# Linear attention: one PSUM tile of four banks for the scores of four heads, and one masked copy of 512 columns

## The chip, the cores and the metric

The kernel runs on one core of a Trainium2 chip. The metric is the device time of one execution in microseconds. Five engines work side by side, each through its own instruction queue in order: PE (TensorE, matrix products, with its weight loads shown apart as PEld), DVE (VectorE), ACT (ScalarE), POOL (GpSimd) and SP (SyncE, which issues most transfers). An engine waits for another by asking for a value of that engine's counter; whatever stands behind the waiting instruction in its queue waits too.

## The reference

One step of a two-layer backbone. Each layer normalises its input, multiplies it by one input projection, and feeds three groups of heads (a state-space group with a convolution, "SSD"; a gated linear attention, "GLA"; a windowed attention), whose outputs pass one output projection. 17 tiles of 128 tokens go through it: 16 of latent tokens and one of context tokens ("CT"). The change sits in the linear attention, where within a chunk of 64 tokens

```python
tri = jnp.tril(jnp.ones((GLA_CHUNK, GLA_CHUNK), dtype=bool))[None, None, None]
att = jnp.where(tri, jnp.einsum('bcqhd,bcshd->bchqs', q_in, k_in), 0.0)
o_intra = jnp.einsum('bchqs,bcshv->bcqhv', att, v)
```

for 4 heads, in two directions.

## The kernel before

Per layer there are four stages. **GLA** (`gla_group`, line 513) takes groups of two tiles: projections into the PSUM pool "d", then gates, cumulative sums and exponentials on DVE and ACT, then for each tile the scores of four heads (L589, 16 small matmuls), their masked copy to SBUF (L590), the sum of the two directions (L591) and the product with the values (L596). **Attention** (`att_weights`, L842) computes per tile four heads of scores (L854, L856), each followed by a maximum on DVE (L857); after the four, exponentials on ACT (L872). **SSD** interleaves by hand the steps of `ssd_scan` for a tile (decays L1104, masked copy L1105, exponential L1107; states L1123 with their reads L1126 and L1133; outputs L1144 and L1151 with their reads L1152 and, after an addition on POOL at L1153, L1154) with the blocks of `ssd_conv` for the next group: 24 matmuls of the helper `prod` (L281), a first tap on ACT (L1057) and four taps on DVE (L1059). Two convolution blocks in four go into the pool "d", two into the pool "s". **Output** (`out_tile`, L1181) forms a gate product in pool "s", which ACT (L1192) and DVE (L1193) read, and the output products in pool "d".

PSUM has eight banks: pools "d" and "m" with two tiles each and "s" with four. `psum(shape, "s")` serves all four stages: every call makes a new tile in one of the four buffers. Waits are not written in the program. The layer that builds it records which instruction touches which tile, derives the waits, and sets the order on every engine from them by a plan of its own; so a change of what depends on what moves instructions everywhere.

Of the kernel before, what the change touches and what calls it, by code (L numbers as in the profile page):

```python
# [10 lines left out]
F32 = mybir.dt.float32  # L11
# [9 lines left out]
P = 128  # L21
# [57 lines left out]
def hybrid_kernel(ctx, tc, a, o):  # L79
    nc = tc.nc  # L80
    V, S, G, T, D = nc.vector, nc.scalar, nc.gpsimd, nc.tensor, nc.sync
# [9 lines left out]
    psp = ctx.enter_context(tc.tile_pool(name="ps", bufs=1, space=PSUM))  # L91
    drp = ctx.enter_context(tc.tile_pool(name="dr", bufs=1, space=DRAM))

    def view(x, shape, dt=F32):

        n = math.prod(shape[1:])
        if dt in (BF16, F16):
            x = x[0:shape[0], 0:(n + 1) // 2].bitcast(dt)[:, 0:n]
        else:
            x = x[0:shape[0], 0:n]  # L100
        if len(shape) == 3:
            x = x.rearrange("p (a b) -> p a b", a=shape[1])
        elif len(shape) == 4:
            x = x.rearrange("p (a b c) -> p a b c", a=shape[1], b=shape[2])
        elif len(shape) == 5:
            x = x.rearrange("p (a b c d) -> p a b c d", a=shape[1], b=shape[2], c=shape[3])
        return x
# [14 lines left out]
    def rot(xs, key):  # L122
        turn[key] = turn.get(key, -1) + 1
        return xs[turn[key] % len(xs)]

    def sb(tag, shape, dt=F32):
        if tag not in where:
            return small.tile(shape, dt, tag=tag, name=tag, bufs=1 if tag in ONCE else 2)
        ph, off, words, n = where[tag]
        off += words * rot(range(n), tag)  # L130
        return view(home.get(ph, work)[:, off:off + words], shape, dt)

    def arena(x):
# [9 lines left out]

        return take

    def psum(shape=None, tag="m"):
        return psp.tile(shape or [P, 512], F32, tag=tag, name="p" + tag, bufs={"d": 2, "m": 2, "s": 4}[tag])


    K = arena(big.tile([P, C_END + 3348 + 12 + 52 * NTT + 162 * L], F32, name="K"))  # L150
# [6 lines left out]
    gmask = cb[:, C_GM:C_GM + 128].bitcast(I32)  # L157
# [61 lines left out]
    def all_sum(src):  # L219

        pr = psum()
        T.matmul(pr[:, 0:1], lhsT=ones, rhs=src, start=True, stop=True)
        return pr[:, 0:1]
# [67 lines left out]
    def hcol(t):  # L291
        return HC if t == CT else 16 + t * P
# [220 lines left out]
    def gla_group(l, s, g):  # L513
# [6 lines left out]
        h = HT[:, :, :, hcol(tiles[0]):hcol(tiles[0]) + W]  # L520
# [52 lines left out]
        qi = sb("gqi", [P, 2, 256])  # L573
# [3 lines left out]
        ki = sb("gki", [P, 2, 256])  # L577
        V.tensor_tensor(ki[:, :, :W], qk[:, 1:2, :W].to_broadcast([P, 2, W]), e2[:, :, :W], ALU.mult)

        for i, t in enumerate(tiles):  # L580
            ax = rot(s.am, "am")
            tx = rot(s.at, "at")
            for hh in range(4):
                hp = slice(32 * hh, 32 * hh + 32)
                pa = psum([P, 2, 64], "s")
                for d in range(2):
                    for c in range(2):
                        ts = slice(i * P + 64 * c, i * P + 64 * c + 64)
                        T.matmul(pa[64 * c:64 * c + 64, d], lhsT=ki[hp, d, ts], rhs=qi[hp, d, ts], start=True, stop=True)  # L589
                V.copy_predicated(ax[:, hh], gmask.rearrange("p (d s) -> p d s", d=2), pa)  # L590
            V.tensor_tensor(tx, ax[:, :, 0], ax[:, :, 1], ALU.add)  # L591
            po = psum()
            for hh in range(4):
                for c in range(2):
                    cs = slice(64 * c, 64 * c + 64)
                    T.matmul(po[cs, 64 * hh:64 * hh + 64], lhsT=tx[cs, hh], rhs=v[cs, i, 64 * hh:64 * hh + 64], start=True, stop=True)  # L596
            oi = sb("goa", [P, 256])
            S.copy(oi, po[:, 0:256])
            D.dma_start(oacc[t], oi)
            for hh in range(4):  # L600
                D.dma_start(sqin[t][hh // 2, 64 * (hh % 2):64 * (hh % 2) + 64].rearrange("(d k) s -> k d s", d=2), qi[32 * hh:32 * hh + 32, :, i * P:(i + 1) * P])
# [8 lines left out]
        for c in range(2):  # L610
            pst = psum([P, 2, 2, 64])
            cs = slice(64 * c, 64 * c + 64)
            for i in range(n):
                for d in range(2):
                    for hh in range(4):
                        T.matmul(pst[32 * hh:32 * hh + 32, d, i], lhsT=kt[cs, i, d, 32 * hh:32 * hh + 32],
                                 rhs=v[cs, i, 64 * hh:64 * hh + 64], start=True, stop=True)
# [813 lines left out]
def build(shapes, consts):  # L1431
    import concourse.bacc as bacc

    nc = bacc.Bacc("TRN2", target_bir_lowering=False, num_devices=1, dynamic_dma_scratch_size=1024)
    f32 = mybir.dt.from_np(np.dtype("float32"))
    a = {n: nc.dram_tensor(f"in_{n}_dram", s, f32, kind="ExternalInput").ap() for n, s in shapes.items()}
    for n, x in consts.items():
        a[n] = nc.dram_tensor(f"in_{n}_dram", x.shape, f32, kind="ExternalInput").ap()
    depth = shapes["w_in"][0]
    outs = {  # L1440
        "y_prompt": shapes["x_prompt"], "y_sample": shapes["x_sample"],
        "new_cache_k": (1, depth, P, 2, 64), "new_cache_v": (1, depth, P, 2, 64),
        "new_state_ssd": (1, depth, 2, 8, 64, P), "new_state_gla": (1, depth, 2, 4, 32, 64),
    }
    o = {n: nc.dram_tensor(f"out_{i}_dram", outs[n], f32, kind="ExternalOutput").ap() for i, n in enumerate(_OUTS)}
    with tile.TileContext(nc, schedule_with_timeline_sim=True) as tc:
        hybrid_kernel(tc, a, o)
    return nc
# [15 lines left out]
```

## Time and profile before

| | us |
|---|---|
| time, median of 3 runs (lowest, highest) | 2300.2 (2296.73, 2302.02) |
| profiled execution, its time | 2304.28 |
| its span | 2302.5 |
| PE busy | 2080.7 (90%) |
| DVE busy | 1628.4 (71%) |
| ACT busy | 992.4 (43%) |
| POOL busy | 878.6 (38%) |

The stages lie, in the first layer, at about 90 to 335 us (GLA), to 615 (attention), to 930 (SSD) and to 1250 (output); in the second at 1250 to 1435, to 1690, to 2010 and to the end. "PEclk" in the profile is the granted clock of PE, 1.00 for 2.4 GHz and 0.50 for 1.2 GHz.

### The profile page before, as it was taken

What the parts mean: (1) busy time and instruction counts of PE and PEld (TensorE: products, weight loads), DVE (VectorE), ACT (ScalarE), POOL (GpSimd) and SP (SyncE); (2) the same over time, 40 slices, a digit from 0 to 9 for tenths busy, and PEclk for the clock granted to TensorE, in tenths of its full rate; (3) what the DMA queues carried; (4) which work ended last, traced back from release to release, by engine and by line L of the source; (5) the groups of instructions that cost most, each with busy time, mean ns of one, the idle gap of its engine ahead of it and who ended that gap; (6) DMA issues with size and microseconds to landing.
All of it is one profiled execution on the core that took longest, in us unless ns stands there. A gap on an engine that the chain in (4) does not pass through costs nothing. (4 is left out here: it accounts for less than half of the span.)

```text
span 2302.5 us, 53686 instructions
## 1 busy us (share of the span) xinstructions
PE 2080.7 (90%) x21228; PEld 1750.4 (76%) x21245; DVE 1628.4 (71%) x4088; ACT 992.4 (43%) x2185; POOL 878.6 (38%) x918
## 2 busy tenths in 40 slices
PE   2596888999899899998999999899999999989998
PEld 0364767778688788887888887777888778878887
DVE  2465768887599988666665657898779988854442
ACT  2333554665444434433333554666563433422221
POOL 0010015556434354544442003566643344444442
PEclk6797979999899999999999999999999999999999
DMA  8687434576710112676667123556751101265553
GB/s 298 165 263 158 121 103 92 124 154 143 168 58 33 38 38 91 183 199 163 168 160 201 41 69 100 122 125 149 160 139 43 38 33 42 81 182 164 154 146 96
DMA packets 486352, 288.01 MB, mean 125 GB/s; under 512 B 354344, under 2 KB 447924, under 8 KB 483796
## 3 DMA queue, kind: packets, MB, share of 16 engines
q1 hardware_dynamic: 483796, 271.99, 45.4%
q0 software_dynamic: 2304, 12.58, 1.8%
q8 instruction: 167, 2.74, 0.5%
q14 instruction: 85, 0.70, 0.1%
HBM read 141.11 MB, written 64.93 MB: 89 GB/s over the span
## 5 line engine op out<-in xcount | busy, mean ns | idle before, releaser
L281 PEld LDWEIGHTS <-HT 128*128 128x128 f16 x6528 | 583.6, 99 | 128.3 <-issue 50.7
L281 PEld LDWEIGHTS <-slot 128*128 128x128 f16 x4320 | 402.3, 98 | 107.5 <-issue 31.3
L281 PE MATMUL pd<-slot,HT 128*128 128x256 f16 x3456 | 430.8, 279 | 10.3 <-DVE work L728 8.0
L281 PE MATMUL pd<-slot,work 128*128 128x256 f16 x3264 | 366.8, 273 | 8.0 <-DMA work<-work 7.7
L281 PEld LDWEIGHTS <-work 128*128 128x128 f16 x3264 | 319.6, 98 | 50.2 <-DMA work<-work 9.1
L281 PE MATMUL pd<-HT,slot 128*128 128x260 f16 (+3 forms) x2592 | 318.0, 270 | 15.7 <-DMA HT<-work 14.5
L281 PE MATMUL ps<-HT,slot 128*128 128x260 f16 (+1 forms) x1728 | 202.8, 272 | 4.8 <-DVE work L1059 4.8
L281 PE MATMUL ps<-slot,HT 128*128 128x256 f16 x1440 | 169.6, 275 | 17.7 <-ACT work L1192 17.7
L1252 POOL TENSOR_TENSOR work<-work 128x512 f32<-128x512 f32 x68 | 90.1, 1325 | 185.5 <-DVE work L1251 156.2
L875 POOL TENSOR_TENSOR work<-work 128x512 f16<-128x512 f32 (+2 forms) x102 | 123.3, 1211 | 86.0 <-ACT work L874 70.8
L1059 DVE SCALAR_TENSOR_TENSOR work<-ps,work 128x256 f32<-128x256 f32 (+1 forms) x288 | 133.3, 464 | 9.1 <-ACT work L1057 4.6
L793 POOL TENSOR_TENSOR work<-work 128x384 f32<-128x384 f32 x34 | 30.2, 889 | 276.1 <-ACT work L789 174.4
L1059 DVE SCALAR_TENSOR_TENSOR work<-pd,work 128x256 f32<-128x256 f32 (+1 forms) x288 | 132.1, 463 | 3.0 <-ACT work L1057 0.3
L872 ACT ACTIVATE work<-ps,nm,K 128x512 f32<-128x512 f32 (+2 forms) x136 | 100.6, 742 | 54.7 <-DVE nm L864 39.3
L1120 POOL TENSOR_TENSOR work<-work 128x512 f32<-128x512 f32 x68 | 72.3, 1068 | 112.6 <-ACT work L1079 67.6
L1061 ACT ACTIVATE work<-work 128x256 f32<-128x256 f32 (+1 forms) x144 | 58.1, 403 | 123.4 <-DVE work L1059 87.4
L854 PEld LDWEIGHTS <-work 128*128 128x128 f16 x1008 | 71.5, 99 | 41.8 <-issue 34.4
L1218 ACT ACTIVATE work<-work 128x512 bf16<-128x512 f32 x68 | 42.7, 628 | 138.3 <-DMA work<-work 75.5
L1093 POOL TENSOR_TENSOR work<-K,work 128x512 bf16<-128x512 bf16 x68 | 73.5, 1081 | 73.7 <-PE ps L1104 63.8
L874 ACT CAST work<-work 128x512 f16<-128x512 f32 (+2 forms) x136 | 78.0, 586 | 52.3 <-DMA slot<-work 31.4
L281 PE MATMUL pm<-slot,HT 128*128 128x256 f16 x816 | 96.1, 275 | 1.6 <-DVE work L907 1.3
L854 PE MATMUL ps<-work 128*128 128x128 f16 x752 | 76.2, 223 | 21.8 <-DMA work<-work 21.8
(375 smaller groups left out, 4029.2 us busy)
## 6 DMA issues: line engine op xcount, KB each, us to landing
slot<-in_w_in_dram SPq DMA_DIRECT2D x24, 1024.0 KB
ymix<-work SPq DMA_DIRECT2D x68, 128.0 KB
yacc<-work SPq DMA_DIRECT2D x34, 256.0 KB
work<-ymix SPq DMA_DIRECT2D x34, 256.0 KB
work<-yacc SPq DMA_DIRECT2D x34, 256.0 KB
x<-work SPq DMA_DIRECT2D x17, 512.0 KB
work<-x SPq DMA_DIRECT2D x17, 512.0 KB
out_dram<-work SPq DMA_DIRECT2D x17, 512.0 KB
```

The source lines that it names most:

```text
L281: T.matmul(out, lhsT=lhs(i, k), rhs=rhs(j, k), start=(n == 0), stop=(n == 3 * KB - 1))
L793: G.tensor_tensor(sq, x, x, ALU.mult)
L854: T.matmul(ps[:, bs], lhsT=s.qt[t][:, 2 * gg + kv], rhs=kt[:, 2 * kv + j], start=(j == 0), stop=(j == 1 and mk is None))
L872: S.activation(pr, sc[hh][:, :nb * P], AF.Exp, scale=s.isc[:, 0:1], bias=nm[:, hh:hh + 1], accum_out=ls[:, hh:hh + 1])
L874: S.copy(p16[:, 0], pr)
L875: (G if hh else V).tensor_tensor(p16[:, 1], pr, p16[:, 0], ALU.subtract)
L1059: V.scalar_tensor_tensor(acc[:, jj, :W], pp[:, q:q + W], s.cw[j][:, q, jj:jj + 1], acc[:, jj, :W], ALU.mult, ALU.add)
L1061: S.activation(th[:, :W], acc[:, jj, :W], AF.Tanh)
L1093: G.tensor_tensor(sr[:, j:j + 4], oh[:, j:j + 4].unsqueeze(2).to_broadcast([P, 4, P]), at.unsqueeze(1).to_broadcast([P, 4, P]), ALU.mult)
L1120: G.tensor_tensor(xw, x, bc8(s.wst[:, t, 8 * d:8 * d + 8]), ALU.mult)
L1218: S.activation(junk, ym[:, 512 * i:512 * i + 512], AF.Square, accum_out=ss[:, i:i + 1])
L1252: G.tensor_tensor(xs[:, js], xs[:, js], tm, ALU.add)
```

## The change

```diff
+    four = psp.tile([P, 4, 512], F32, tag="s", name="four", bufs=1)
+
     def psum(shape=None, tag="m"):
-        return psp.tile(shape or [P, 512], F32, tag=tag, name="p" + tag, bufs={"d": 2, "m": 2, "s": 4}[tag])
+        if tag == "s":
+            return view(rot([four[:, i] for i in range(4)], "four"), shape or [P, 512])
+        return psp.tile(shape or [P, 512], F32, tag=tag, name="p" + tag, bufs=2)
...
             for hh in range(4):
                 hp = slice(32 * hh, 32 * hh + 32)
-                pa = psum([P, 2, 64], "s")
                 for d in range(2):
                     for c in range(2):
                         ts = slice(i * P + 64 * c, i * P + 64 * c + 64)
-                        T.matmul(pa[64 * c:64 * c + 64, d], lhsT=ki[hp, d, ts], rhs=qi[hp, d, ts], start=True, stop=True)
-                V.copy_predicated(ax[:, hh], gmask.rearrange("p (d s) -> p d s", d=2), pa)
+                        T.matmul(four[64 * c:64 * c + 64, hh, 64 * d:64 * d + 64], lhsT=ki[hp, d, ts], rhs=qi[hp, d, ts], start=True, stop=True)
+            V.copy_predicated(ax.rearrange("p h d s -> p h (d s)"), gmask.unsqueeze(1).to_broadcast([P, 4, P]), four[:, :, 0:P])
```

Two things change. For each tile and layer one masked copy of 4 x 128 columns stands in place of four of 128: 34 on DVE in place of 136. And the four buffers of the pool "s" become the four banks of one tile, `four`, which is made once and never released; every user of "s" in the four stages gets the next bank of it in turn. The matmuls are as many as before (35219 instructions on PE in both built programs). From L147 on a line of the kernel before stands four lines further down in the changed one; the text uses the numbers of before.

In the built program the waits of PE on readers of this PSUM tile are others than before. Each wait was followed to the instruction at which the other engine's counter reaches the asked value. Before, a matmul that writes an "s" buffer waits for the readers of that same buffer. Now it waits for the readers of any bank of `four` that stand ahead of it in the program. Some counts of PE's waits, by the line that writes and the line that it waits for: L854 for L857 0 before, 102 now; L854 for L872 126 before, 32 now; L281 for L1154 1 and 30; L281 for L1107 12 and 30; L1104 for L1107 0 and 32; L1144 for L1133 0 and 32; L1123 for L1059 10 and 30.

PE in the SSD stage, from the output matmuls (L1144, L1151; 1148 and 1155 in the changed kernel) to the next convolution block in "s". `HT` is the normalised input, the slots hold weights; DVE_49 and Activation_49 are the counters of DVE and ACT. Before:

```order
L281 LDWEIGHTS slot_71
L281 MATMUL pd<-HT,slot_71 128x260
L1151 MATMUL ps<-K,work 128x256 [waits DVE_49]
L1151 MATMUL ps<-K,work 128x256
L281 LDWEIGHTS slot_72
L281 MATMUL ps<-HT,slot_72 128x260 [waits Activation_49]
```

and now:

```order
L1148 MATMUL four<-work 128x64 [waits DVE_49]
L1148 MATMUL four<-work 128x64 x7
L1155 MATMUL four<-K,work 128x256 x2
L285 LDWEIGHTS slot_67
L285 MATMUL four<-HT,slot_67 128x260 [waits DVE_49]
```

Before, the block's first matmul waits for ACT's read of an earlier buffer (L1126). Now it waits for L1154, the last read of the outputs that the rows just above it write.

PE in the SSD stage, from a convolution block in "s" to the decays (L1104; 1108 now) and on to the next block. Before:

```order
L1104 LDWEIGHTS work
L1104 MATMUL ps<-work 128x512
L1104 LDWEIGHTS work
L1104 MATMUL ps<-work 128x512 [waits DVE_49]
L281 LDWEIGHTS slot_67
L281 MATMUL pd<-HT,slot_67 128x260
```

and now:

```order
L285 LDWEIGHTS slot_68
L285 MATMUL four<-HT,slot_67 128x260
L1108 LDWEIGHTS work [waits DVE_49]
L1108 MATMUL four<-work 128x512 [waits Activation_49]
L1108 LDWEIGHTS work
L1108 MATMUL four<-work 128x512
L1081 MATMUL pm<-K,work 128x128 [waits DVE_49]
L1086 MATMUL pm<-K,work 128x128 [waits DVE_49,Activation_49]
L1108 LDWEIGHTS work
L1108 MATMUL four<-work 128x512 [waits Activation_49]
L1108 LDWEIGHTS work
L1108 MATMUL four<-work 128x512
```

The first decays now wait for the four taps (L1059) of the block just above, the second pair for the exponential (L1107) of the first, and the 24 matmuls of a block in `four` that follow (not shown) for the exponential of the second.

PE in the attention stage, between two heads of one tile (L854 and L856; 858 and 860 now). Before:

```order
L854 LDWEIGHTS work [waits DMAHW5_49,DMAHW4_49]
L854 MATMUL ps<-K,work 128x128 [waits Activation_49]
L854 LDWEIGHTS work
L854 MATMUL ps<-K,work 128x128
L854 LDWEIGHTS work
L854 MATMUL ps<-work 128x128
L854 LDWEIGHTS work
L854 MATMUL ps<-work 128x128
L854 LDWEIGHTS work
L854 MATMUL ps<-K,work 128x128 [waits Activation_49]
```

and now:

```order
L858 LDWEIGHTS work
L858 MATMUL four<-work 128x128
L860 LDWEIGHTS K
L860 MATMUL four<-K 128x128
L858 LDWEIGHTS work
L858 MATMUL four<-K,work 128x128 [waits DVE_49]
L858 LDWEIGHTS work
L858 MATMUL four<-K,work 128x128
```

Before, a head waits for the exponential (L872) of the earlier tile that used its buffer. Now it waits for the maximum (L857) of the head just before it, and the first head of a tile for the last exponential of the tile before.

## Rows read from the trace of the kernel before

**Rows 1.** The page, part 1: busy time, share of the span, instructions of each engine.

```profile
PE 2080.7 (90%) x21228; PEld 1750.4 (76%) x21245; DVE 1628.4 (71%) x4088; ACT 992.4 (43%) x2185; POOL 878.6 (38%) x918
```

**Rows 2.** Busy time by stage: stretch, length, engines, PEclk, DMA share, GB/s.

```profile
335.00:615.00 280.00, 251.70 (x2645) 213.73 (x2642) 224.48 (x556) 159.35 (x376) 158.10 (x178) 0.97 0.61 135
615.00:930.00 315.00, 302.06 (x2497) 256.05 (x2504) 274.83 (x708) 135.60 (x308) 130.55 (x123) 0.98 0.20 62
1250.00:1435.00 185.00, 179.02 (x2922) 150.01 (x2921) 117.59 (x374) 97.38 (x224) 16.44 (x18) 0.98 0.29 80
1435.00:1690.00 255.00, 229.81 (x2491) 195.73 (x2488) 209.88 (x514) 151.60 (x354) 153.45 (x169) 0.99 0.64 138
1690.00:2010.00 320.00, 308.92 (x2526) 262.94 (x2533) 279.41 (x714) 136.13 (x309) 132.47 (x125) 0.98 0.18 57
```

**Rows 3.** Waits of PE for others: us in total, times, longest.

```profile
PE ps L281 <- ACT work L1192: 17.7, 10, 3.3
PE ps L854 <- ACT work L872: 9.8, 11, 2.2
PE ps L281 <- DVE work L1059: 4.8, 2, 2.4
PE ps L589 <- DVE work L590: 4.3, 3, 3.7
PE ps L1104 <- DVE ps L1105: 1.3, 2, 0.9
```

**Rows 4.** Lines with shapes apart: busy us, mean ns; the masked copies.

```profile
L590 DVE COPY_PREDICATED work<-K,ps 128x128 f32<-128x128 int32 x136 | 33.4, 296 | 25.2 <-PE ps L589 25.0
L1105 DVE COPY_PREDICATED ps<-K,ps 128x512 f32<-128x512 int32 x68 | 46.6, 685 | 0.2
```

**Rows 5.** Timeline of a GLA tile: start, length, engine, line.

```profile
1336.70 0.89 DVE L590 COPY_PREDICATED work<-K,ps 128x128 f32<-128x128 int32 x4
```

**Rows 6.** Lines with shapes apart: readers of "s" in the SSD stage, and one transpose.

```profile
L1057 ACT ACTIVATE work<-ps,work 128x256 f32<-128x256 f32 x64 | 35.7, 558 | 46.5 <-PE ps L281 46.3
L1107 ACT ACTIVATE work<-ps 128x512 f32<-128x512 f32 x68 | 40.5, 595 | 72.9 <-DVE ps L1105 70.9
L1133 DVE TENSOR_TENSOR K<-ps,K 128x512 f32<-128x512 f32 x32 | 21.8, 680 | 0.6 <-PE ps L1123 0.6
L1152 DVE TENSOR_TENSOR work<-ps,K 128x512 f32<-128x512 f32 x32 | 21.9, 683 | 5.1 <-PE ps L1151 5.1
L1153 POOL TENSOR_TENSOR work<-work 128x512 f32<-128x512 f32 x32 | 42.6, 1333 | 15.8 <-issue 14.9 <-POOL K L1132 0.9
L1154 DVE TENSOR_TENSOR work<-ps,work 128x512 f32<-128x512 f32 x32 | 21.9, 685 | 21.1 <-POOL work L1153 21.1
L1082 PE MATMUL pm<-K,work 128*128 128x128 f32 x68 | 16.6, 274 | 1.6 <-DVE work L1062 1.6
```

**Rows 7.** Timeline of the SSD stage: one convolution block on PE, four taps on DVE.

```profile
1923.43 2.86 PE L281 MATMUL ps<-HT,slot 128*128 128x260 f16 x24
1928.10 2.03 DVE L1059 SCALAR_TENSOR_TENSOR work<-ps,work 128x256 f32<-128x256 f32 x4
```

**Rows 8.** Lines with shapes apart: the maximum of one head in the attention.

```profile
L857 DVE TENSOR_REDUCE mx<-ps 128x1 f32<-128x512 f32 x112 | 73.3, 679 | 5.3 <-PE ps L856 5.0
```

**Rows 9.** Timeline of one attention tile, from its maxima to its last exponential.

```profile
1571.40 0.16 DVE L864 TENSOR_SCALAR nm<-nm 128x4 f32<-128x4 f32 x1
...
1576.03 0.78 ACT L872 ACTIVATE work<-ps,nm,K 128x512 f32<-128x512 f32 x1 [0.52 <-POOL work L875]
```

**Rows 10.** Three stretches of 8 us, columns as in Rows 2.

```profile
402.00:410.00 8.00, 5.59 (x69) 4.74 (x64) 5.60 (x17) 7.90 (x15) 2.48 (x2) 1.00 0.50 61
482.00:490.00 8.00, 5.69 (x55) 4.22 (x53) 5.60 (x12) 4.93 (x9) 3.63 (x3) 0.79 0.95 162
586.00:594.00 8.00, 5.43 (x35) 4.02 (x35) 2.59 (x6) 0.85 (x2) 3.06 (x6) 0.59 0.52 103
```

## The prediction

> **What bounds the kernel now.** I read the page first: PE is busy 90% of the span, DVE 71% [rows 1]. Shares of the whole hide the stages, so next the busy time by stage [rows 2]. In both SSD stages PE is busy 302 of 315 and 309 of 320 us, and in the second GLA stage 179 of 185: nothing there moves the end but PE's own work and new holes in it. In the attention stages PE is busy 252 of 280 and 230 of 255 us, with DVE next (224 and 210), so 28 and 25 us of holes exist already. DVE's 279 of 320 us in the second SSD stage is the second thing to watch. The third view is what PE waited for [rows 3]. Waits on readers of the tiles "ps" are a few microseconds each: 17.7, 9.8, 4.8, 4.3, 1.3, some 38 us together. Four buffers are enough today: PE fills one while DVE and ACT read others.
>
> **The change part by part.** *The masked copies.* Four of 128 columns take 0.89 us from the first start to the last end [rows 5], since they overlap (each alone 296 ns [rows 4]). One copy of 512 columns with a PSUM input and a mask isn't in this trace; the nearest row is the masked copy L1105 of the same size, 685 ns [rows 4], which also writes to PSUM. The floor is one short copy, 296 ns, the ceiling the four in a row, 890 ns. I take 685, so DVE saves 0.2 us a tile, 34 x 0.2 = 7 us, with 0 to 20 us as bounds. That time is in the GLA stages, where PE and not DVE is the limit, so on the path I count 0. The copy now starts after 16 matmuls instead of 4; PE has projection products queued behind, so that costs nothing unless those run out.
>
> *The waits.* This is what the change really moves. A matmul that writes any bank of `four` waits for the readers of all banks that stand ahead of it. The program alternates write, read, write, read, so what overlapped across four buffers is now a chain, unless PE has other work queued between. I went along PE's queue in the changed order. At each such wait I set the length of the read against the PE work that stands between the last write and the waiting matmul. A convolution block is 24 matmuls in 2.86 us [rows 7]; where a block for pool "d" lies between, the wait costs nothing, since no read there is longer. The reads, all in the SSD stage:
> - A convolution block in `four` is read by a first tap on ACT, 558 ns [rows 6], and four taps on DVE that depend on each other, 2.03 us [rows 7]: 2.6 us. At 29 of 30 states (L1123) behind a block, at most two or three small matmuls of about 0.27 us [rows 6] stand between: 29 x 2.5 = 73 us. At 16 of 32 first decays (L1104) nothing does: 16 x 2.6 = 42 us.
> - The outputs L1144 and L1151 are read by DVE, POOL and DVE again, 683 + 1333 + 685 ns [rows 6] = 2.7 us. In 16 of 30 places the next block follows at once, and in 2 more the decays: 18 x 2.7 = 49, less a little, 48 us.
> - A pair of decays is read by the masked copy, 685 ns [rows 4], and the exponential, 595 ns [rows 6]: 1.28 us. In 28 of 30 places a block follows at once: 36 us. In 19 of 34 the second pair follows the first with one or two transposes between: 19 x 1.05 = 20 us.
> - The states are read by L1133 in 680 ns [rows 6]; in 16 of 32 places 0.45 us of it is uncovered: 7 us. A few odd places add 8.
>
> The SSD sum is 73 + 42 + 48 + 36 + 20 + 7 + 8 = 234 us for both layers, 14 us for a group of two tiles.
>
> *Attention.* The next head waits for the maximum, 679 ns [rows 8]. Of 90 such waits 33 have too little PE work between: 22 us. The first head of a tile waits for the last exponential, which ends 5.3 us after the start of L864 (1576.81 less 1571.56, its end) and so some 6 us after the last maximum starts [rows 9]. 10 of 30 places lack on average 1.4 us: 14 us, with 4 more at one odd place: 40 us. These stages have 53 us of PE holes already [rows 2], and a new hole may lie in an old one; I count half, 20 us, between 0 and 40. *GLA.* The copy's 0.69 us has 32 matmuls, 3.8 us at the rate of [rows 7], before it is needed; a few places lack cover: 3 us. *Output.* The two readers of the gate product now hold the next tile's gate product. A tile's output products, 96 matmuls or 11 us, lie between: 0. Without that cover it would be some 1.2 us on each of 34 tiles, by the lengths of [rows 6].
>
> *What durations alone do not show.* Read by durations, the order of before leaves PE 1.5 us of waits on "ps", and the trace has 38 [rows 3]: the readers stand in queues behind other work. DVE carries the weight splits in the SSD stages as well. I add 40 us, between 0 and 80. Of the 24 us of PE holes in the SSD stages [rows 2] I take back 12. *The clock.* A PE that stops often may be granted less. Three stretches with PE busy 68 to 71% ran at 1.00, 0.79 and 0.59 of 2.4 GHz [rows 10]. The SSD stages will be some 70% busy (305 of 430 us a layer). At full clock this costs 0; at the mean of the three, 0.79, their 611 us of PE work would take 162 us more. Their holes are mostly shorter than 3 us, as in the stretch that stayed at 1.00: I take 30.
>
> Sum: 234 + 20 + 3 + 40 - 12 + 30 = 315 us on the profiled execution's 2304.3 us, 2619; the median of the runs shown is 4 us lower, so **2615 us**.
>
> **The rivals.** *The banks stay independent in effect* (the other side): each new wait falls on a read that is already over. It decides where the PE work between a write and the next one is longer than the read, as in GLA. Then the 7 us of DVE time are all that is left, between off the path and wholly on it: 2293 to 2300 us. Against it stand the orders printed above, where the waiting matmul follows the awaited write at once. The Trainium skill, page "PSUM — Partial Sum Buffer", section "Summary: rules for kernel authors", has a rule for this side: read one bank while a matmul writes another, and guard PSUM by bank. By that rule one tile of four banks loses nothing, and the time would be this rival's; the waits in the built program do not go by banks, and no row of before can show what that costs.
>
> *PE finds other work.* The plan that set the order is not the chip's timing, and holes may merge with holes of DMA and DVE that exist: half of the SSD sum goes, the attention and queue terms vanish: 2304 + 60 to 170 = 2365 to 2470 us. For it speak the 222 us that PE is idle now (2302.5 less 2080.7 [rows 1]); against it, only 24 of them lie in the SSD stages [rows 2].
>
> *The clock falls for good in SSD.* If half of PE's time there were granted 1.2 GHz (mean 0.75), its 611 us would take 204 us more; with the other terms 2304 + 285 + 204 = 2790 us. The stretches at 0.79 and 0.59 speak for it [rows 10], the one at 1.00 against. The Trainium skill, page "TensorE: Matmul & The Clock Gate", section "Part 1: The HAM clock gate", says that the lower clock is the default and activity lifts it; the rows agree that both levels occur at this share of work.
>
> **How the numbers follow.** The forecast holds 80%: its range of 2475 to 2760 us has at its foot the SSD sum less all 24 us of old holes and a sixth of it merged away, with no attention, queue or clock term, and at its head 80 for queues, 40 for attention and the clock at some 0.85. Banks independent: 4%, half of it faster by more than 0.2%, half within 0.2% (about what a measurement here tells from no change). Other work found: 7%. Clock low throughout: 9%. Left out of the range are 20%. Faster 0.02, same 0.02, slower 0.96.
>
> **What would show it.** In the profile after, PE busy in the SSD stages should fall from 96% to about 70% while GLA and output keep their length. PE's waits should name L1059, L1154 and L1107 as the longest, near 115, 48 and 56 us before queues, and L857 in attention. A group of two SSD tiles should take about 14 us longer or more. DVE busy should fall by some 7 us in L590 with 34 copies near 0.7 us. The prediction is wrong if PE waits for these lines stay below 100 us in total, if the SSD stages keep 315 and 320 us, or if PEclk there falls under 0.8.

## The result and the profile after

The changed kernel takes 3030.1 us (median; 3015.0 to 3039.7) where the kernel before takes 2298.5 us in the same session (2287.7 to 2302.0). The ratio is 1.322, with a 95% interval of 1.318 to 1.327. The prediction of 2615 us had the sign right and the size wrong: of 732 us of loss it foresaw 315, and the time lies above its range of 2475 to 2760.

The page of the profiled execution after the change (its time 3015.0 us, its span 3012.8 us): the busy time of PE, its busy tenths in 40 slices, and the granted clock in the same slices. It answers [rows 1].

```profile
PE 2339.4 (78%) x21212; PEld 1881.2 (62%) x21245; DVE 1650.3 (55%) x3986; ACT 1005.3 (33%) x2183; POOL 865.9 (29%) x918
```

```profile
PE   3778677778677766699998978787766777768999
...
PEclk6889799888777787799999979898887777778999
```

Two things are to be seen. PE is busy 78% of a span that is 710 us longer. And its busy time, in itself, grew from 2080.7 to 2339.4 us, although the products are the same. So there are two losses: 452 us in which PE stands still, and 259 us in which the same work takes longer. The last row points at the reason: the granted clock stands mostly at 0.7 or 0.8 in the slices in which PE is busy for 0.6 to 0.7 of the time, and mostly at 0.9 where it is busy for 0.9.

To see the stages I cut both traces at the same events: the first maximum of a layer (L857 before, L861 after), the last one, the last sum of an output (L1154, L1158), and the last product with the output gate in layer one (L1251, L1255). This differs from the round cuts of [rows 2]. Columns as there: the stretch, its length, busy time of PE, PEld, DVE, ACT and POOL with their instructions, PEclk, DMA share, GB/s. The kernel before: attention, SSD and output of the first layer, then GLA, attention and SSD of the second.

```profile
334.60:605.30 270.70, 244.36 (x2551) 207.44 (x2549) 216.38 (x536) 154.05 (x366) 154.52 (x175) 0.97 0.60 132
605.30:952.20 346.90, 331.96 (x2768) 282.42 (x2774) 301.52 (x784) 151.81 (x341) 144.31 (x137) 0.99 0.23 71
952.20:1245.00 292.80, 274.09 (x2433) 241.28 (x2431) 189.32 (x365) 100.65 (x184) 130.67 (x130) 0.99 0.67 179
1245.00:1412.90 167.90, 161.89 (x2731) 135.96 (x2731) 100.24 (x324) 86.26 (x195) 7.14 (x9) 1.00 0.30 82
1412.90:1676.80 263.90, 238.58 (x2571) 202.58 (x2569) 217.50 (x535) 154.60 (x368) 159.13 (x176) 0.97 0.62 136
1676.80:2020.30 343.50, 331.78 (x2774) 283.26 (x2781) 300.51 (x774) 152.75 (x342) 143.95 (x135) 0.99 0.21 63
```

The changed kernel, the same six stages:

```profile
336.70:688.70 352.00, 270.99 (x2663) 226.10 (x2663) 219.46 (x555) 163.35 (x377) 157.05 (x181) 0.88 0.47 109
688.70:1291.10 602.40, 425.73 (x2649) 322.64 (x2667) 318.05 (x774) 152.31 (x337) 139.96 (x132) 0.79 0.13 40
1291.10:1583.90 292.80, 276.89 (x2459) 243.99 (x2458) 181.56 (x358) 98.96 (x181) 124.67 (x129) 0.99 0.65 174
1583.90:1792.50 208.60, 173.72 (x2783) 142.85 (x2786) 104.85 (x281) 88.61 (x199) 11.13 (x13) 0.90 0.25 68
1792.50:2134.20 341.70, 276.10 (x2742) 231.28 (x2739) 218.56 (x570) 161.38 (x377) 157.36 (x177) 0.89 0.47 110
2134.20:2732.80 598.60, 419.67 (x2518) 316.39 (x2533) 309.64 (x735) 146.78 (x326) 138.61 (x130) 0.78 0.11 33
```

Read a pair of rows as a ledger. The first SSD stage grew from 346.9 to 602.4 us. PE's idle time in it (length less busy) grew from 14.9 to 176.7 us, and its busy time from 332.0 to 425.7 us. Multiply busy time by granted clock, as if the mean of the stage held while PE is busy: 332.0 x 0.99 = 329 before, 425.7 x 0.79 = 336 after. The work is the same within 2%, so nearly all of the 94 us of extra busy time are the clock. The output stage has kept its 292.8 us. Over both layers (first GLA stage and last output stage from the same views):

| stages | idle, change | busy, change | together | predicted, without clock |
|---|---|---|---|---|
| SSD | +329 | +182 | +511 | +262 (234 + 40 - 12) |
| attention | +95 | +64 | +159 | +20 |
| GLA | +36 | +7 | +43 | +3 |
| output | -8 | +6 | -2 | 0 |
| sum | +452 | +259 | +710 | +285, and 30 for the clock |

The waits of PE in the changed kernel (who waits, for whom: us in total, times, longest), against [rows 3]:

```profile
PE four L1127 <- DVE work L1063: 63.8, 23, 2.8
PE four L285 <- ACT work L1111: 60.8, 28, 2.6
PE four L1108 <- DVE work L1063: 51.5, 26, 2.7
PE four L285 <- DVE work L1158: 49.2, 16, 3.6
PE pm L896 <- DMA slot<-work: 36.4, 20, 7.9
PE pm L896 <- DMA work<-work: 33.3, 20, 7.5
PE four L858 <- DVE mx L861: 27.8, 35, 3.2
PE four L858 <- ACT work L876: 25.4, 9, 8.4
PE pm L1081 <- DVE work L1066: 24.8, 22, 3.8
...
PE four L1148 <- DVE K L1137: 18.3, 14, 4.0
PE four L593 <- DVE work L582: 18.1, 4, 6.1
```

The first four rows are waits that the prediction priced. Kind by kind: states on the taps 63.8 us (predicted 73), decays on the taps 51.5 (42), blocks on exponentials 60.8 (36). Blocks on outputs are 49.2, with two decays on outputs (8.3, in a row not shown) 57.5 (48). Decays on decays, predicted at 20 us, are 4.9 (not shown either). Together these kinds are 238.5 us where the prediction had 219. Four other rows the prediction did not have: two waits on the transposing DMA (L896), one on the product behind the tanh (L1066), one in GLA on the keys (L582).

Lines with shapes apart, of the changed kernel: a matmul of a convolution block in `four`, and the masked copy.

```profile
L285 PE MATMUL four<-HT,slot 128*128 128x260 f16 x1536 | 262.5, 347 | 110.7 <-ACT work L1111 60.8 <-DVE work L1158 49.2 <-DVE work L1063 0.6
L594 DVE COPY_PREDICATED work<-K,four 128x512 f32<-128x512 int32 x34 | 24.6, 724 | 48.5 <-PE four L593 48.5
```

The same matmul in the kernel before:

```profile
L281 PE MATMUL ps<-HT,slot 128*128 128x260 f16 x1536 | 188.5, 276 | 4.8 <-DVE work L1059 4.8
```

One and the same matmul went from 276 to 347 ns on the mean. The copy did what the change says: 34 of 724 ns, 24.6 us, instead of 33.4 us [rows 4]. DVE saves 9 us there, where PE and not DVE is late.

### The profile page after: what moved, and what is told of

Its sections match the earlier page's. It is cut to its first block, busy times and chain, and to the rows that moved or that the text cites. A ratio compares the mean times of both kernels' runs of the same rounds, so it can differ in the third digit from the quotient of the medians.

```text
span 3012.8 us, 53638 instructions
## 1 busy us (share of the span) xinstructions
PE 2339.4 (78%) x21212; PEld 1881.2 (62%) x21245; DVE 1650.3 (55%) x3986; ACT 1005.3 (33%) x2183; POOL 865.9 (29%) x918
## 5 line engine op out<-in xcount | busy, mean ns | idle before, releaser
L285 PEld LDWEIGHTS <-slot 128*128 128x128 f16 x4320 | 443.9, 108 | 270.4 <-issue 145.6
L285 PE MATMUL four<-HT,slot 128*128 128x260 f16 (+1 forms) x1728 | 276.9, 334 | 110.7 <-ACT work L1111 60.8
L285 PE MATMUL pd<-HT,slot 128*128 128x260 f16 (+3 forms) x2592 | 306.6, 274 | 26.1 <-DMA HT<-work 10.8
L1063 DVE SCALAR_TENSOR_TENSOR work<-four,work 128x256 f32<-128x256 f32 (+1 forms) x288 | 134.5, 467 | 237.4 <-ACT work L1061 231.8
L285 PE MATMUL four<-slot,HT 128*128 128x256 f16 x1440 | 168.8, 274 | 16.0 <-ACT work L1196 15.3
L1061 ACT ACTIVATE work<-four,work 128x256 f32<-128x256 f32 (+1 forms) x72 | 39.7, 552 | 410.6 <-PE four L285 410.5
L1127 PE MATMUL four<-work 128*128 128x256 f32 x272 | 109.3, 574 | 81.7 <-DVE work L1063 63.8
L1256 POOL TENSOR_TENSOR work<-work 128x512 f32<-128x512 f32 x68 | 88.7, 1304 | 199.3 <-DVE work L1255 160.5
L1063 DVE SCALAR_TENSOR_TENSOR work<-pd,work 128x256 f32<-128x256 f32 (+1 forms) x288 | 132.0, 465 | 20.2 <-ACT work L1061 15.3
L861 DVE TENSOR_REDUCE mx<-four 128x1 f32<-128x512 f32 (+2 forms) x136 | 88.1, 648 | 96.3 <-PE four L860 82.4
L1127 PEld LDWEIGHTS four<-work 128*128 128x128 f32 x272 | 73.8, 282 | 106.5 <-issue 91.8
L1151 POOL TENSOR_TENSOR work<-work 128x512 f32<-128x512 f32 x34 | 36.5, 1073 | 335.8 <-PE four L1127 300.7
L876 ACT ACTIVATE work<-four,nm,K 128x512 f32<-128x512 f32 (+2 forms) x136 | 100.6, 742 | 77.8 <-DVE nm L868 56.4
```

The costliest lines, as they stand in the source:

```text
L285: T.matmul(out, lhsT=lhs(i, k), rhs=rhs(j, k), start=(n == 0), stop=(n == 3 * KB - 1))
L861: V.tensor_reduce(mx[:, hh:hh + 1], ps[:, :nb * P], AX.X, ALU.max)
L876: S.activation(pr, sc[hh][:, :nb * P], AF.Exp, scale=s.isc[:, 0:1], bias=nm[:, hh:hh + 1], accum_out=ls[:, hh:hh + 1])
L1061: S.activation(acc[:, jj, :W], pp[:, 0:W], AF.Identity, scale=s.cw[j][:, 0, jj:jj + 1], bias=s.cbias[:, b:b + 1])
L1063: V.scalar_tensor_tensor(acc[:, jj, :W], pp[:, q:q + W], s.cw[j][:, q, jj:jj + 1], acc[:, jj, :W], ALU.mult, ALU.add)
L1127: T.matmul(pp[:, 256 * g:256 * g + 256], lhsT=bt[:, g], rhs=xw[:, 4 * g:4 * g + 4].rearrange("p h d -> p (h d)"), start=True, stop=True)
```

## The experiments

The verdict of each run is its ratio to the kernel before on the same chip, with the 95% interval.

### The tile or the copy

**Four copies again, the tile as changed.** The edit against the changed kernel:

```diff
+                pa = psum([P, 2, 64], "s")
...
-                        T.matmul(four[64 * c:64 * c + 64, hh, 64 * d:64 * d + 64], ...
+                        T.matmul(pa[64 * c:64 * c + 64, d], ...
-            V.copy_predicated(ax.rearrange(...), gmask...to_broadcast([P, 4, P]), four[:, :, 0:P])
+                V.copy_predicated(ax[:, hh], gmask.rearrange("p (d s) -> p d s", d=2), pa)
```

> The four-bank tile `four` of the changed kernel, but each head is masked by its own copy of 128 columns again, as in the kernel before. Theory A (one tile for the four banks makes a chain of write, read, write, read among all its users; the copy plays no part): the time stays at 3000 to 3060 us, ratio 1.31 to 1.33, and the SSD stages stay near 600 us at a granted clock near 0.79. Rival B (the loss comes from the one copy of 512 columns that waits for sixteen matmuls and reads four banks): back to 2290 to 2310 us. If both play a part the time lies clearly between.

Measured: 3110.0 us, ratio 1.358 (1.350 to 1.366), above the 3060 us that I named for theory A. The copy is cleared of the loss, but it does play a part, and helps: with the tile alone the loss is larger by 0.036 of 2290 us, some 82 us. Its second GLA stage, beside the 208.6 us above:

```profile
1637.30:1893.20 255.90, 217.82 (x2779) 170.08 (x2782) 114.56 (x338) 90.34 (x201) 12.30 (x15) 0.81 0.20 56
```

and a row of its waits of PE:

```profile
PE four L594 <- DVE work L595: 27.0, 53, 1.6
```

In one shared tile each head's scores wait for the copy of the head ahead; one copy for four heads takes three of these four waits away. What these waits cost is mostly not idle time: of the 47 us by which this stage is longer than the 208.6 us, 3 are idle time of PE and 44 busy time, at a granted clock of 0.81 where the changed kernel has 0.90. The gain of the copy is a gain only against this tile. With four separate tiles that wait was 4.3 us in all [rows 3].

**Two tiles of two banks.**

```diff
+    two = [psp.tile([P, 2, 512], F32, tag=f"s{i}", name=f"two{i}", bufs=1) for i in range(2)]
...
+            return view(rot([two[i % 2][:, i // 2] for i in range(4)], "four"), shape or [P, 512])
```

> The four banks as two tiles of two banks, used in turn, so a write waits for the readers of the last user but one instead of the last; four copies of 128 as before. Theory A: most reads of 0.7 to 2.7 us are then covered by the work of the user between (a convolution block is 2.86 us), so the 325 us of new idle time in SSD fall to a third or less: 2330 to 2500 us, with the granted clock in SSD above 0.9. Rival C (any tile that holds more than one bank costs the same, however many): near 3030 us. Rival B (the copy alone): 2290 to 2310 us.

Measured: 2723.0 us, ratio 1.188 (1.179 to 1.196). This is a dose: with four short copies each time, four tiles of one bank give 1, two of two banks 1.188, one of four banks 1.358. But my number was too low by over 220 us. The first SSD stage:

```profile
652.00:1170.10 518.10, 404.16 (x2671) 303.05 (x2671) 309.04 (x774) 152.47 (x338) 141.97 (x135) 0.84 0.14 44
```

PE is idle for 114 of 518 us, not for a third of 177. I had taken it that the work of one user covers the read of the other. The row of waits that is longest shows where it does not:

```profile
PE two L1109 <- DVE work L1064: 46.1, 19, 2.7
```

The two tiles go by turns in the order of the program, and PE's queue has another. In the first SSD stage eight decays (L1109 here) that use the same tile as a block stand right behind that block on the queue and wait 2.7 us each for its taps, the whole length of the read.

The Trainium skill, page "PSUM — Partial Sum Buffer", section "Summary: rules for kernel authors", advises reading one bank while a matmul writes another, with guards by bank. No run here contradicts the first half; the three doses show what becomes of it when the guard is the tile.

**No convolution block in the tile.** In the changed kernel, and as a control in the kernel before:

```diff
-                pp = psum(None, rot(('d', 's'), "cps"))
+                pp = psum(None, 'd')
```

> The changed kernel, but every convolution block takes a buffer of pool `d` instead of every second one a bank of `four`. Theory A: PE's waits of the decays and the states on the taps (63.8 and 51.5 us in the changed kernel) and of the blocks on exponentials and outputs (60.8 and 49.2 us) all have a convolution block in `four` on one side, and go; what is left in SSD are decays on decays and outputs on states. SSD 380 to 450 us a layer instead of 601, clock above 0.9, total 2600 to 2750 us, with attention unchanged at 350 us. Rival D (the clock falls in SSD for a reason other than these waits): the waits go but the clock stays near 0.79, SSD 480 us or more a layer and the total above 2790 us.

> Control for e4_conv_d: the kernel before with every convolution block in pool `d`. Two buffers for blocks of 2.86 us whose readers take 2.6 us should be enough: 2290 to 2340 us by every theory. If it is much slower, e4_conv_d pays for that too and has to be read against this one.

Measured: 2608.8 us, ratio 1.140 (1.133 to 1.147), for the changed kernel, and 2356.2 us, ratio 1.029 (1.022 to 1.036), for the control. The first SSD stage of the former:

```profile
693.00:1098.60 405.60, 344.48 (x2657) 280.99 (x2658) 308.83 (x772) 148.50 (x335) 143.03 (x132) 0.93 0.19 58
```

One user fewer in the tile gives 197 us of 255 back in this stage, and the granted clock goes from 0.79 to 0.93. Beside the control, whose first SSD stage is 379.6 us long, 26 us of loss are left. Attention keeps its loss (348.6 and 336.2 us long). The control shows that two buffers for all blocks are not free: 66 us, more than I allowed.

### Which chain costs what

The next nine kernels are the kernel before, with its four rotating tiles and four copies, and some of the waits of the changed kernel written in by hand. A wait of this kind is one line, here from attention:

```diff
-                    T.matmul(ps[:, bs], lhsT=s.qt[t][:, 2 * gg + kv], ...)
+                    w = T.matmul(ps[:, bs], lhsT=s.qt[t][:, 2 * gg + kv], ...)
+                    if b == 0 and j == 0 and hh:
+                        after_read(w, last["m"])
...
-            V.tensor_reduce(mx[:, hh:hh + 1], ...)
+            last["m"] = V.tensor_reduce(mx[:, hh:hh + 1], ...)
```

**Attention.** First the wait of a head for the maximum ahead, then that of a tile's first head for the last exponential, then both.

> The kernel before, with its four rotating tiles, and one wait of the changed kernel put in alone: in attention the first matmul of a head waits for the maximum of the head ahead of it. Theory P (my prediction: each wait costs what PE work does not cover, and a new hole may lie in an old one): +11 to +22 us, 2295 to 2325 us. Theory Q (the wait also lengthens the way of a tile to its transposing DMA and lowers the granted clock): +30 to +70 us, attention stages 285 to 300 us long at a clock near 0.94.

> The kernel before and the other wait of attention alone: the first matmul of a tile's first head waits for the last exponential of the tile ahead. Theory P: +9 to +18 us, 2293 to 2320 us. Theory Q (this wait is the larger one, since it holds up all four heads and with them the transposing DMA of the tile): +70 to +130 us, and PE's waits on the transposing DMA grow from 12 us to over 40.

> The kernel before with both waits of attention, and nothing else of the change. If attention lost its 159 us by these two waits alone, its stages take 345 to 355 us a layer here too at a clock of 0.88 to 0.89, and the time is 2435 to 2465 us. Theory P: +20 to +40 us, 2305 to 2340 us. Rival R (attention lost by what the SSD and GLA chains leave behind, or by another user of the tile): under +80 us.

Measured: 2349.3 us, ratio 1.023 (1.019 to 1.028); 2308.7 us, 1.005 (1.002 to 1.008); both 2436.6 us, 1.061 (1.057 to 1.065). In microseconds 53, 13 and 141. The first attention stage of the first kernel, of the second and of the third:

```profile
312.50:618.50 306.00, 260.09 (x2608) 217.41 (x2606) 223.09 (x550) 159.05 (x369) 151.72 (x178) 0.94 0.54 122
```

```profile
317.70:594.10 276.40, 245.40 (x2554) 207.78 (x2552) 216.69 (x535) 153.54 (x366) 158.72 (x176) 0.95 0.58 130
```

```profile
335.30:679.10 343.80, 273.02 (x2631) 224.71 (x2629) 216.36 (x553) 162.42 (x373) 161.24 (x182) 0.90 0.47 111
```

So the two waits are nearly all that attention lost (141 of 159 us; the two attention stages of the third kernel, 343.8 and 350.9 us, are by themselves 160 us longer than before). The wait for the maximum alone costs what theory Q gave it, the wait for the exponential alone no more than theory P did. Together they cost twice their sum, which neither had. The waits of PE with both name where the rest went, first with both waits,

```profile
PE pm L902 <- DMA slot<-work: 38.1, 21, 4.9
PE ps L860 <- DVE mx L867: 28.7, 33, 3.4
PE pm L902 <- DMA work<-work: 22.0, 12, 3.4
```

then in the kernel before:

```profile
PE pm L892 <- DMA work<-work: 6.4, 6, 1.9
PE pm L892 <- DMA slot<-work: 6.0, 3, 3.0
```

The value products (L902, L892 before) wait for the transposing DMA of the probabilities: 60 us instead of 12 (29 with the wait for the maximum alone, 20 with the wait for the exponential alone). With one of the two waits in place a tile is late, but the next can still run ahead; with both, the scores of a tile come after the exponentials of the one ahead and its transposes later still. That reading fits the rows; it was not tested by moving the DMA.

**SSD.** First the waits on the taps of a block, then the waits of a block on the others, then these two together, then the whole chain (with decays on decays, outputs on states and decays on outputs).

```diff
+    def user(kind, w):
+        for k, r in last:
+            if k == "conv":
+                tc.add_manual_dep(w.ins, r.ins.name, mybir.DependencyInfo(mybir.DependencyClass.Sync, ...))
+        last.clear()
```

`user` stands at the first matmul of each step that writes pool "s", and `last` holds the reads of the tile ahead (`read`). In the second kernel the condition is `kind == "conv" and k != "conv"`, in the third `(k == "conv") != (kind == "conv")`, in the fourth there is none.

> The kernel before, four rotating tiles, with one kind of wait of the changed kernel put in alone: in SSD the first decay, state or output matmul after a convolution block in pool `s` waits for that block's last tap. My sum gave these waits 73 + 42 = 115 us. Theory Sum (waits add up, and the clock takes a part on top): 2410 to 2460 us, each SSD stage about 60 us longer, clock there near 0.95. Theory Q (alone a wait is mostly absorbed because the other steps can still run ahead; only the closed chain costs the whole): 2325 to 2375 us.

> The kernel before with the other half alone: a convolution block in pool `s` waits for the reads of the decays, states or outputs that stand ahead of it (exponential, sum of the output). My sum gave these 36 + 48 = 84 us. Theory Sum: 2380 to 2425 us. Theory Q: 2310 to 2345 us.

> The waits of s1_taps and of s2_blocks together in the kernel before, without the steps of the chain that neither had (decays on decays, outputs on states, decays on outputs). Alone they cost 157 and 91 us, the whole chain of SSD 472 us. Theory Sum (waits add up; the rest of the 472 us belongs to the steps left out): 2296 + 157 + 91, 2520 to 2570 us. Theory Q (the two together close the chain, and it is the closed chain that costs): 2620 us or more.

> The kernel before with the whole chain of SSD put in, each user of pool `s` there waiting for the readers of the user ahead of it; attention, GLA and output as before. If the chain is the whole of what SSD lost, its stages take 590 to 610 us a layer at a granted clock of 0.78 to 0.80, as in the changed kernel, and the time is 2780 to 2830 us. Rival R (the shared tile costs SSD something besides these waits): under 530 us a layer, under 2660 us.

Measured: 2452.4 us, ratio 1.069 (1.065 to 1.072); 2386.3 us, 1.040 (1.036 to 1.044); the two together 2620.3 us, 1.143 (1.138 to 1.148); the whole chain 2767.9 us, 1.204 (1.198 to 1.210). That is 157, 91, 328 and 472 us. The first SSD stage in that order:

```profile
591.60:1015.70 424.10, 365.79 (x2780) 301.15 (x2778) 302.66 (x783) 153.25 (x341) 141.32 (x136) 0.92 0.19 58
```

```profile
593.80:993.60 399.80, 347.35 (x2810) 288.39 (x2808) 303.21 (x784) 153.76 (x342) 144.04 (x138) 0.97 0.21 62
```

```profile
594.40:1105.70 511.30, 401.41 (x2776) 314.77 (x2774) 312.14 (x783) 154.60 (x341) 143.21 (x136) 0.85 0.16 48
```

```profile
599.30:1182.20 582.90, 429.31 (x2752) 321.95 (x2750) 314.63 (x788) 157.15 (x342) 141.25 (x136) 0.81 0.14 43
```

Idle time of PE beyond the 14.9 us of before: 43, 38, 95 and 139 us in this layer. Taps and blocks alone give 81; together 95; the steps left out bring 44 more. Idle time thus nearly adds up. The clock does so less, 0.92 and 0.97 alone, 0.85 and 0.81 together: busy time beyond 332.0 us is 34, 15, 69 and 97 us. Over both layers idle time of the two together is 29 us above the sum of the two alone, and busy time 56 us. Theory Sum holds for each half alone, and fails by 80 us for the two together; 2620.3 us lies on the edge of what theory Q named. In both layers the whole chain makes 272 us of idle time (139 here, 133 in the second layer), where the prediction had 262. Its stages, 583 and 577 us, are a little shorter than I named, and hold 469 of the 511 us that SSD lost.

**GLA.** The same, with `user` at the scores and at the transposes of the gate inputs and of the keys, and `read` at the last masked copy of a tile and at the copy of the keys.

> The kernel before with the chain in GLA alone: scores wait for the last masked copy of the tile ahead, the transposes of the keys for the last masked copy, the next group's first transpose for the copy of these. The second GLA stage lost 41 us, where I had counted 3 for both. Theory R (the chain does it): that stage 195 to 212 us, clock 0.89 to 0.95, total 2325 to 2350 us. Rival C (the one copy after sixteen matmuls, or the changed order, does it): the stage keeps 168 us and the total 2290 to 2305 us.

Measured: 2364.6 us, ratio 1.029 (1.027 to 1.032). The second GLA stage:

```profile
1264.50:1478.10 213.60, 175.32 (x2730) 143.63 (x2730) 108.41 (x331) 87.97 (x197) 9.70 (x12) 0.88 0.24 66
```

It is 46 us longer than before (a little more than I named), so the chain does it, without the single copy. The wait that grew most is not one of the chain:

```profile
PE ps L602 <- DVE work L591: 37.7, 10, 6.1
```

The scores (L602 here) wait for the keys with their gate (L591), the end of a long row of steps on DVE and ACT that begins with the transpose of the gate inputs (L550). That transpose comes late: other products stand ahead of it on PE's queue, so PE hardly waits there, but in this stage DVE stands idle for 35.8 us ahead of its copy of these transposes (L554), 4.5 us before (L541). The chain's own waits for the masked copy are smaller, 10.8 us at the scores and 12.4 us at the transposes of the keys. I had looked for cover of the copy only. (The first GLA stage is 311 to 335 us long in kernels that leave it as it was, so in the changed kernel, at 336.7 us, it says little. Here it is 350.2 us, above them all, which fits the part of the 69 us that the second stage does not hold.)

**All three chains.** The waits of the third kernel of attention, the fourth of SSD and that of GLA.

> The kernel before with the chains of GLA, attention and SSD all put in: still four rotating tiles and four masked copies a tile. One after the other they cost 69, 141 and 472 us. If stages add up and the chain is all that the changed kernel lost: 2296 + 682, 2940 to 3020 us, ratio 1.28 to 1.32. Rival R (the shared tile costs something beside the waits, or the chain runs on over the ends of stages): 3030 us or more for the latter; under 2900 us if the chains overlap.

Measured: 2956.9 us, ratio 1.292 (1.286 to 1.299). That is 665 us beside the sum of 69 + 141 + 472 = 682; stages add up. Four tiles and four copies with these waits lose nine tenths of what the changed kernel loses. Between 1.292 and 1.322 some 69 us stay open. They lie in SSD, whose stages are 569.8 and 564.1 us long instead of 602.4 and 598.6; the first has 149 us of idle time here,

```profile
689.20:1259.00 569.80, 420.81 (x2670) 314.70 (x2671) 304.48 (x769) 151.49 (x335) 138.52 (x130) 0.81 0.13 41
```

and 177 in the changed kernel. Part of it is in one row of waits, blocks on exponentials, here

```profile
PE ps L292 <- ACT work L1138: 23.1, 16, 2.4
```

where the changed kernel has 60.8 us in 28 waits: its order puts more blocks behind this read. What else makes the 69 us was not tried.

### Why the clock falls

> The changed kernel with matmuls that nobody reads: twelve of 128x260 into a buffer of pool `d` ahead of each convolution block in `four`, of each tile's first decays, states and outputs, 174 times 12 in all, some 240 us of PE work at full clock, 120 a layer. It tells why the granted clock in SSD fell from 0.99 to 0.79. Theory A (it falls because PE stands still at the new waits): with the holes partly filled the clock rises to 0.9 or more, SSD does 450 us of full-speed work in 520 to 600 us, no longer than the 601 us without the extra work, and the total is 2870 to 3040 us. Rival D (it falls for another reason, which work does not undo): clock stays near 0.79, SSD 640 us or more a layer, total above 3110 us.

> Control for f1_after_fill: the kernel before with the same 174 times 12 matmuls that nobody reads. Where PE has no holes they cost their full length: some 240 us, 2500 to 2560 us, SSD near 465 us a layer at a clock of 0.98 or more. In the changed kernel the same work made the time 35 us shorter. If it costs under 150 us here too, the fill says nothing on the holes.

```diff
+    def fill(n):
+        pf = psum(None, "d")
+        for k in range(n):
+            T.matmul(pf[:, 0:260], lhsT=HT[:, 0, k % KB, 16:16 + P], rhs=HT[:, 1, k % KB, 16:276], start=True, stop=True)
...
+                if tag == "s":
+                    fill(12)
```

Measured: the changed kernel with the fill takes 2995.4 us, ratio 1.306 (1.302 to 1.310), 35 us less than without it. The kernel before with the same fill takes 2504.1 us, ratio 1.092 (1.087 to 1.097), 212 us more than without. The first SSD stage of the changed kernel with the fill, and of the kernel before with it:

```profile
690.30:1283.60 593.30, 496.14 (x3698) 397.95 (x3699) 316.74 (x774) 153.69 (x337) 139.79 (x132) 0.89 0.13 41
```

```profile
592.90:1035.60 442.70, 435.56 (x3746) 375.90 (x3744) 304.82 (x773) 148.99 (x333) 138.51 (x135) 1.00 0.18 56
```

Without holes the fill costs what it is long (this stage is 96 us longer, by 104 us of busy time). With holes it takes 80 us of idle time away (177 to 97 us) and the clock rises from 0.79 to 0.89, a hair under the 0.9 I named. In full-speed work PE does 496.1 x 0.89 = 442 us instead of 336, in a stage that is 9 us shorter. So the clock falls because PE stands still: work that nobody needs, put where PE stood, brings part of it back.

The mechanism is to be seen in small in the changed kernel, in two neighbouring stretches of its first SSD stage,

```profile
780.00:793.00 13.00, 6.71 (x46) 5.03 (x44) 9.68 (x29) 5.17 (x11) 3.26 (x3) 1.00 0.01 2
793.00:807.00 14.00, 9.81 (x40) 7.62 (x41) 3.63 (x7) 3.48 (x12) 3.30 (x3) 0.51 0.10 37
```

and in the timeline of PE (start, length, line, in brackets the idle time ahead): a convolution block of 24 matmuls, and the next one of the same shape in `four`.

```profile
782.41 2.86 PE L285 MATMUL four<-HT,slot 128*128 128x260 f16 x24 [1.08 <-ACT work L1111]
...
803.15 4.58 PE L285 MATMUL four<-HT,slot 128*128 128x260 f16 x24 [3.12 <-DVE work L1158]
```

In the first stretch PE works 6.7 of 13 us, in pieces, still at 2.4 GHz (1.00). Then the clock is at 1.2 GHz nearly throughout (0.51), and a block like the one that took 2.86 us takes 4.58. The Trainium skill, page "TensorE: Matmul & The Clock Gate", section "Part 1: The HAM clock gate", lists these two levels in its table of states, the lower one as the default that activity lifts. The two stretches agree, at 1.00 and 0.51, and by that rule the means of 0.79 or 0.88 are shares of time at the two. In SSD, with its many short stops, the lower level costs 182 us.

## Why the prediction was wrong

**The chain: right, and its terms right in the sum.** Writes to a bank wait for the readers of all banks, and the users of pool "s" form a chain. The kernel with two tiles of two banks and the one with the waits written in by hand show it. The five kinds of wait priced in the order measured 238.5 us against 219. That the waits on the taps came to 115 us, as predicted, is luck: states were 9 us too high, decays 10 us too low. Blocks on exponentials were mis-sized most, 36 us against 60.8 measured, 28 waits as counted but 2.2 us each and not 1.28. The order on PE's queue, read with durations of the trace, is good for the sum of the first round of waits, not for each.

**SSD, the idle time: nearly right.** 262 us predicted (with 40 for queues and less 12 of old holes), 272 in the kernel with the chain alone, 329 in the changed kernel. The 40 us for queues were a guess, and it holds in the sum alone. A part of the miss is in blocks on exponentials, and a part in the term for outputs on states, 7 us, whose wait measured 18.3 (L1148).

**The clock: the step that failed most.** "Their holes are mostly shorter than 3 us, as in the stretch that stayed at 1.00: I take 30." It measured 259 us, of them 182 in SSD. [rows 10] had three stretches with PE busy some 70%; I went by the one that suited the forecast. Their mean, 0.79, is what SSD was granted (0.79 and 0.78). That value, 162 us, stood in the text. It would have given 2747 us, at the head of the range. A term that multiplies all of PE's work in a stage is not one to set by one row in three. The list of signs did name it: the prediction is wrong "if PEclk there falls under 0.8".

**Attention: 20 us predicted, 159 measured.** The failed step is "a new hole may lie in an old one; I count half". The two waits themselves measured 27.8 and 25.4 us, not far from the 40 before halving. (The 5.3 us in that term run from the end of L864, not from its start as the text has it; that is 0.2 us at each of 10 places.) One old wait of PE was indeed absorbed, that of the scores for a DMA; this row of the kernel before has no like in the changed one:

```profile
PE ps L854 <- DMA work<-work: 21.8, 13, 3.6
```

But idle time still grew by 95 us. What came on top was the next wait behind the two, on the transposing DMA (69.7 us instead of 12.4), and the clock (64 us). I had priced a wait by how late PE starts the next step and not by what that step feeds.

**GLA: 3 us predicted, 43 measured.** The failed step is "a few places lack cover: 3 us". It looked at the copy alone. In the changed kernel PE's waits for the copy are 15.1 us (L610 9.9, L593 5.2; 4.9 before), so even its cover had more gaps. And the transposes at the head of the next group stand in the chain too: a late transpose makes late keys, for which the scores wait 18.1 us (L593, L582; 4.1 before).

**The masked copy: right.** 724 ns against 685, 9 us of DVE against 7, off the path. That it would matter only through the tile it shares was not foreseen: against four copies in the same tile it saves 82 us.

**Output: right.** No change, by the cover named: the gate product's wait for its reader on ACT is 15.3 us, 17.7 before [rows 3].

**The rivals.** Independent banks and other work for PE were wrong. "The clock falls for good in SSD", 2790 us at 9%, had the mechanism and in SSD nearly the size (0.75 against 0.785). It too lacked attention, GLA and the clock outside SSD. The range ended at a clock of about 0.85 and 40 us of attention; both bounds were too near.

Keeping one copy without the shared tile was not tried: all four heads would have to write one bank, which no run here does. No run here points to a kernel faster than the one before, in which PE waits for that copy for 4.3 us in all [rows 3].

## What to carry over

Before several banks are joined in one tile to save an instruction, ask whether the waits go by bank or by tile, and go through all the users of the pool, not only the one that is edited. Price a new wait in three parts: the hole on the waiting engine, the next thing that becomes late behind it, and, on TensorE, the clock that the whole stage loses; here the idle time was 452 us, of which 285 were foreseen, and the clock took 259 us, of which 30 were foreseen. Waits tried one at a time can look harmless (53 and 13 us) and cost 141 together.

## What the runs showed of the hardware

I had not expected that stops of one to four microseconds take so much of the granted clock: with PE idle for 29% of a stage the clock was 0.79 (SSD after the change), for 23% 0.88 (attention), for 22% 0.84 (pairs of banks), for 15% 0.93 (no blocks in the tile), for 4% 0.99 (SSD before). The share alone does not set it: attention with 23% was granted more than the pairs with 22%. Nor that extra matmuls can shorten a kernel: some 212 us of them made the changed kernel 35 us faster.
